# Reordering the RWKV-7 scan pipeline: group norm and gate behind the inverse's first levels, low-rank products ahead of them, fp32 head sums

## The chip, the cores and the metric

The kernel runs on one core of one Trainium2 chip. The metric is device time in microseconds, from the launch's start on the device to its end; lower is better. One execution was also recorded by the hardware profiler.

## What is computed

A two-layer decoder trunk on 16 meta tokens and 256 tokens (272 columns), width 2048, everything in fp32. Layer 0 is RWKV-7 time mixing and a SwiGLU block; layer 1 is stick-breaking attention with a shared K/V and another SwiGLU block. The change lies inside the time mixing:

```python
w = -softplus(-(dec_w0 + tanh(xw @ dec_w1) @ dec_w2)) - 0.5
decay = exp(-exp(w))
a = sigmoid(a_w0 + (xa @ a_w1) @ a_w2)
g = sigmoid(xg @ g_w1) @ g_w2
kk = normalised per head (k * k_k);  k = k * (1 + (a - 1) * k_a)
# per token and head, state 64 x 64
sa    = state @ (-kk)
state = state * decay + sa (kk * a)^T + v k^T
y     = state @ r
# group norm per head, bonus, gate, output projection
y = (y - mean) * rsqrt(var + GN_EPS) * gn_w + gn_b
bonus = sum_head(r * k * r_k) * v
out = ((y + bonus) * g) @ w_o
```

## The kernel before

**Layout.** Activations stand transposed: channels on the 128 partitions, the 272 tokens along the free axis. 2048 channels are 16 slabs, and a slab holds two heads of 64, a "pair". Matrix products against large weights split each fp32 operand into a high and a low part in the reduced format fp32r and add three products (`mm3k`, lines 186 to 188); the weight slabs are split on the chip by a cast on ACT (`whi`, L703) and a subtraction on DVE (`wlo`, L704).

**The scan.** The recurrence is done in chunks: 16 meta tokens, then four chunks of 64. `scan` runs a software pipeline over the 16 pairs, `n` from -3 to 15. In one iteration four pairs are in four different stages:

- C = pair n+3: `lora` (decay and learning rate from the low-rank products, the running decay `L` by a scan on DVE, its exponentials `P`, `Q` and `pe`, then the products `AR0`, `ARV`, `B0`, `BK`).
- B = pair n+2: `chunk0`, `scores`, `neg`, `bonus`, `tokens`, `values`, and `solve`, which inverts the 16 x 16 diagonal blocks on POOL.
- M = pair n+1: `inverse` (two DMA hops through DRAM that bring the solved blocks back as `Tt`), then the two doubling levels `left(16)`, `right(16)`, `left(32)`, `right(32)`, then `apply` and `trans`. `left` transposes `Tt` into `Tn` on DVE and multiplies `yb`; DVE masks it into `Ys`; `right` multiplies `zb` from `Tn` and `Ys`, and DVE adds it to `Tt`.
- A = pair n: `states`, `step(1..4)` (the state passes from chunk to chunk), `norm` (group norm), `gate` (the product `gp` and the output slab `o`).

Between these stages `f(k)` lets PE do k steps of a background stream of large products, one step being the three matmuls of one 128 x 128 weight block (the `w_v` and `w_r` projections of pair n+3, and at the end the first part of `w_o`): 32 steps in a full iteration. While three pairs are left there is no C, and `f` does half as many. The last step of the v projection calls `after_v`, that of the r projection `after_r`.

**What sets the order.** PE and the SP DMA queue run in program order (`manual_schedule`). DVE, ACT and POOL are ordered at compile time by a planner that takes the program's order as priority; each engine then runs its list in that order. One order is written by hand: in `left`

```python
with b.tc.issue_after(b.last.ins):
    V.transpose(self.Tn.rearrange(flat), Tt[:, :4].rearrange(flat))
```

puts the transposition behind the DVE instruction that `b.last` names. `bonus` sets it to its product `bv`, and `gate` sets it again, to the instruction that writes `o`. The order of the calls is `bonus`, `f(2)`, `tokens`, `lora`, `f(3)`, `norm`, `f(1)`, `gate`, `f(3)`, `left(16)`, `values`, `solve`, `f(4)`, `right(16)` and so on.

**Small products.** The per-head sums (`head_sums`: `bonus` and the variance `vb`) multiply a 0/1 block matrix by an operand that ACT and DVE split into high and low first (`high_low`, L996 and L998): two fp32r matmuls each. The low-rank weights of a pair come in two loads (`load_lora`, `load_gate`) and are split where they are used (`split_w`, L989 and L990). PSUM tiles of the scan come from three tags of two banks in rotation (`rbank`). Several SBUF tiles share a buffer through `ALIAS`.

Of the kernel before, what the change touches and what calls it, by code (L numbers as in the profile page):

```python
# [18 lines left out]
NK = D // 128  # L19
# [17 lines left out]
CONST = {}  # L37
ALIAS = {"kk": "ld", "v": "L", "sq": "Mp", "rs2": "Rh", "y": "Ah"}
NRAW = 3
# [79 lines left out]
class Builder:  # L119
# [195 lines left out]
    def vectors(self):  # L315
        nc = self.nc
        self.dvec = {"hdw0": 0, "ha0": NK, "oka": 2 * NK, "mg0": 9 * NK}
        self.dvec.update({f"om{i}": (3 + i) * NK for i in range(6)})
        self.dvec.update(hka=10 * NK, mgn=11 * NK)
# [3 lines left out]
        nc.vector.memset(self.dv[:, b + 2:b + 3], 1.0)  # L323
        self.eps = self.dv[:, b:b + 1]
# [10 lines left out]
        nc.vector.tensor_scalar(self.dv[:, 2 * NK:3 * NK], v16("k_a"), -1.0, 1.0,  # L335
                                ALU.mult, ALU.add)
        o = self.dvec["mgn"]
        nc.vector.tensor_scalar(self.dv[:, o:o + NK], v16("gn_w"), -0.5, None, ALU.mult)
        nc.vector.tensor_scalar(self.dv[:, 3 * NK:9 * NK], self.vecs[:, 0:6 * NK], -1.0, 1.0,
# [8 lines left out]
    def time_mix(self):  # L348
# [13 lines left out]
        with ExitStack() as ctx:  # L362
# [18 lines left out]
            o, n = CONST["blk"]  # L381
            raw = sp.tile([128, 5, 64], F32, name="blk", tag="Tt", bufs=BUFS["Tt"])
            raw = raw.rearrange("p c t -> p (c t)")[:, :n]
            self.dq.dma_start(raw, a["consts"][:, o:o + n])
            self.blk = []
            for i, x in enumerate((1.0, 1.0 / HD)):
                t = sp.tile([128, n], F32R, name="blk", tag=f"blk{i}")
                nc.scalar.activation(t, raw, AF.Copy, scale=x)
                self.blk.append(t)
            with tc.manual_schedule(engines={mybir.EngineType.PE, mybir.EngineType.SP}):  # L390
# [213 lines left out]
    def scan(self, sp):  # L604
# [17 lines left out]

        pairs[0].load_lora()
        for n in range(-3, NK):
            get = lambda i: pairs.get(n + i)
            A, M, B, C = get(0), get(1), get(2), get(3)
            f = fill if C else lambda k: fill(k / 2)
            if M:
                M.inverse()
            if A:  # L630
                A.states()
                A.step(1)
            if B:
                B.chunk0()
            if A:
# [12 lines left out]
            f(2)  # L648
            if B:
                B.tokens()  # L650
            if C:
                C.lora()
            f(3 + (LEAD if n == -3 else 0))
            if A:
                A.norm()
                f(1)
                A.gate()
                f(3)
            else:
                f(4)  # L660
            if M:
                M.left(16)
            if B:
                B.values()
                B.solve()
                if n + 2 == NK - 1:
                    self.rot = self.rot[1:]
            f(4)
            for g in ("right", 16), ("left", 32), ("right", 32), ("apply", None), ("trans", None):
                if M:  # L670
                    getattr(M, g[0])(*g[1:] if g[1] else ())
                f(3 if g[0] == "trans" else 4)
                if g == ("left", 32):
                    if M:
                        M.load_gate()
                    if get(4):
                        get(4).load_lora()

# [267 lines left out]
class Pair:  # L946
# [20 lines left out]

    def load_w(self, lo, hi):

        raw = self.b.l2.tile([128, hi - lo], F32, name="w2", tag="w2", bufs=2)  # L970
        self.nc.sync.dma_start(raw, self.b.a["lora2"][self.p][:, lo:hi])
        return raw

    def load_lora(self):
        p = self.p
        self.da = self.load_w(0, 256)
        self.rn = self.t272("rn")
        self.nc.sync.dma_start(
            self.rn, self.b.rkd[2 * p:2 * p + 2].unsqueeze(1).to_broadcast([2, 64, T]))

    def load_gate(self):
        self.g = self.load_w(256, 512)

    def split_w(self, raw, name):
        b = self.b
        n = raw.shape[1]
        h = b.l2.tile([128, n], F32R, name=name + "h", tag=name + "h", bufs=1)
        l = b.l2.tile([128, n], F32R, name=name + "l", tag=name + "l", bufs=1)
        self.A.copy(h, raw)  # L989
        self.V.tensor_tensor(l, raw, h.bitcast(F32), ALU.subtract)  # L990
        return (h[:, :128], l[:, :128]), (h[:, 128:], l[:, 128:])

    def high_low(self, x):
        b = self.b
        hi = b.rstd_p.tile([128, T], F32R, name="hi", tag="rstd")
        self.A.copy(hi, x)  # L996
        lo = b.rstd_p.tile([128, T], F32R, name="lo", tag="rstdt")
        self.V.tensor_tensor(lo, x, hi.bitcast(F32), ALU.subtract)  # L998
        return hi, lo

    def head_sums(self, name, block, x):

        out = self.b.rbank(name)[:, :T]
        self.PE.matmul(out, block, x[0], start=True, stop=False)
        self.PE.matmul(out, block, x[1], start=False, stop=True)
        return out

    def lora(self):

        b, p, V, A, nc = self.b, self.p, self.V, self.A, self.nc  # L1010
        kt = b.k[p]
        wd, wa = [tuple(x[:96] for x in w) for w in self.split_w(self.da, "da")]
        rn = self.rn
# [10 lines left out]
        A.activation(ta, za[:, :T], AF.Tanh, bias=self.vec("ha0"), scale=0.5)  # L1024

        self.P = P = self.t272("P", 17 + 65 * NCH)
        self.Pc = Pc = P[:, 17:].rearrange("p (c t) -> p c t", t=65)
        nc.gpsimd.memset(P[:, 0:1], 1.0)
        nc.gpsimd.memset(Pc[:, :, 0:1], 1.0)
# [7 lines left out]
        V.tensor_scalar(ta, ta, 0.5, 0.5, ALU.mult, ALU.add)  # L1037
        self.k2 = k2 = self.t272("k2")
# [19 lines left out]
        def par(tile, first, second):  # L1058
# [6 lines left out]
                               Pc[:, :, :C], ALU.mult, ALU.mult)  # L1065
        V.tensor_tensor(kk, ta, kk, ALU.mult)
        V.tensor_tensor(self.B0[:, 0:META], kk[:, :META], Q[:, :META], ALU.mult)
# [4 lines left out]
    def after_v(self, vp):  # L1072
        A = self.A
        self.v = v = self.t272("v")
        A.copy(v, vp)
        self.b.dump("v", self.p, v)
        A.copy(self.V0[:, 32:32 + META], vp[:, :META])
        A.copy(self.ARV[:, :, 2], vp[:, META:].rearrange("p (c t) -> p c t", t=C))

    def after_r(self, rp):  # L1080
        V = self.V
        rs = self.t272("rs")
        self.A.copy(rs, rp)
        V.tensor_tensor(self.AR0[:, 1], rs[:, :META], self.P[:, 1:17], ALU.mult)
        V.tensor_tensor(self.ARV[:, :, 0], rs[:, META:].rearrange("p (c t) -> p c t", t=C),
                        self.Pc[:, :, 1:], ALU.mult)
        V.scalar_tensor_tensor(rs, rs, self.vec("r_k"), self.k2, ALU.mult, ALU.mult)
        self.rk = self.high_low(rs)

# [61 lines left out]
    def bonus(self):  # L1151
        bp = self.head_sums("bonus", self.b.blk[0], self.rk)
        self.bv = self.t272("bv")
        self.b.last = self.V.tensor_tensor(self.bv, self.v, bp, ALU.mult)

# [98 lines left out]
    def apply(self):  # L1254
# [12 lines left out]
        for r in range(2):  # L1267
            self.A.copy(X[HS[r], r * 2:r * 2 + 2, 0], wa4[HS[r], :, :, 1])

# [66 lines left out]
    def gate(self):  # L1336
        b = self.b
        w = self.split_w(self.g, "g")
        gp = b.rbank("gp")
        b.mm3k(gp[:, :T], w[0], b.hg[0], True, False)  # L1340
        b.mm3k(gp[:, :T], w[1], b.hg[1], False, True)
        o = b.kp.tile([128, T], F32, name="o", tag="kp")
        b.last = self.V.scalar_tensor_tensor(o, self.y, self.vec("gn_b"), gp[:, :T], ALU.add, ALU.mult)
        b.dump("o", self.p, o)
# [55 lines left out]
```

## Time and profile before

| | us |
|---|---|
| median of 3 runs (2813.58 to 2815.2) | 2813.61 |
| profiled execution, its own time | 2815.13 |
| span, first to last instruction of it | 2813.3 |
| scan stage, from the first pair's `lora` to the last pair's `o` | about 190 to 748 |

| engine | busy us | share of the span |
|---|---|---|
| PE (matmul) | 2688.5 | 96% |
| DVE | 1798.6 | 64% |
| ACT | 1492.6 | 53% |
| POOL | 178.8 | 6% |

PE is busy nearly all of the time, so a stage can only become shorter where PE waits, where its clock is held down, or where it is given less to do. POOL works in the scan alone, so its row in the table of slices marks that stage. The page's matmul durations overlap, since matmuls are pipelined; the distance of the starts is what one costs.

### The profile page before, as it was taken

The page shows a single profiled execution, that of the slowest core. Times are in us where ns is not written, and L with a number is a line of the kernel's source. Part 1 is how long each engine was busy: PE and PEld are TensorE (multiplying, and loading weights), DVE is VectorE, ACT ScalarE, POOL GpSimd, SP SyncE. Part 2 cuts the span into 40 slices and gives each one's busy share as a digit, 9 for nine tenths or more (in the row PEclk, how much of TensorE's full clock was granted, in tenths as well). Part 3 has the DMA queues.
Part 4 walks back from the last instruction along what each step waited for, and adds up shares of the span by engine and source line. Part 5 has one row for each costly group of instructions (what it writes and reads, how often), then busy time and mean ns, then how long its engine had stood idle before and what let it go on. Part 6 is the DMA issues. An engine that isn't in the chain of part 4 may idle for free.

```text
span 2813.3 us, 54147 instructions
## 1 busy us (share of the span) xinstructions
PE 2688.5 (96%) x20942; PEld 2487.2 (88%) x20942; DVE 1798.6 (64%) x3586; ACT 1492.6 (53%) x3005; POOL 178.8 (6%) x539
## 2 busy tenths in 40 slices
PE   7988888888899999999999999999999999999999
PEld 5777777777799999999999999988888888888888
DVE  6656565566465555555555776577776666666666
ACT  6665555555454444444444665467655455455554
POOL 0005333333100000000000000000000000000000
PEclk9999999999899999999999999999999999999999
DMA  5434333332456555555565555533456565665665
GB/s 177 128 104 122 87 84 84 87 91 78 139 165 186 167 184 176 166 184 177 165 184 177 166 173 165 176 131 116 155 187 187 184 193 180 199 189 179 196 185 175
DMA packets 185330, 439.50 MB, mean 156 GB/s; under 512 B 58448, under 2 KB 88688, under 8 KB 185072
## 3 DMA queue, kind: packets, MB, share of 16 engines
q1 hardware_dynamic: 183488, 433.63, 50.0%
q8 instruction: 164, 2.69, 0.4%
q10 hardware_dynamic: 1584, 2.42, 0.3%
q14 instruction: 94, 0.77, 0.1%
HBM read 430.24 MB, written 5.74 MB: 155 GB/s over the span
## 4 chain that ended last, share of the span: by engine, by line
PE 88%; DVE 4%; ACT 3%; DMA 3%; issue 2%; POOL 0%; SPq 0%; ACTq 0%; DVEq 0%
PE mm L192 22%; PE mm L186 16%; PE mm L188 15%; PE mm L187 15%; PE mm L191 11%; PE lr L540 1%; PE zb L1250 1%; DMA raw<-w_k 1%; DMA raw<-w_r 1%; PE cb L1312 1%; PE hms L831 1%; ACT L1030 1%; PE wa L1261 1%; PE yb L1231 1%; PE cb L1304 1%
## 5 line engine op out<-in xcount | busy, mean ns | idle before, releaser
L168 DVE TENSOR_TENSOR wlo<-raw,whi 128x512 fp32r<-128x512 f32 (+1 forms) x1448 | 979.0, 679 | 621.1 <-ACT whi L167 601.4
L167 ACT CAST whi<-raw 128x512 fp32r<-128x512 f32 (+1 forms) x1448 | 879.3, 610 | 877.0 <-PE mm L187 542.2
L186 PE MATMUL mm<-hl,whi 128*128 128x272 f32 x3344 | 976.1, 292 | 13.4 <-ACT whi L703 9.5
L188 PE MATMUL mm<-hl,wlo 128*128 128x272 f32 x3344 | 968.8, 290 | 4.4 <-DVE wlo L168 4.4
L187 PE MATMUL mm<-hl,whi 128*128 128x272 f32 x3344 | 965.5, 289 | 0.0
L192 PE MATMUL mm<-hl,whi 128*128 128x512 f32 x2624 | 919.8, 395 | 0.0
L191 PE MATMUL mm<-hl,wlo 128*128 128x256 f32 x2624 | 740.8, 282 | 0.0
L186 PEld LDWEIGHTS mm<-hl,whi 128*128 128x128 f32 x3344 | 631.5, 189 | 23.9 <-ACT whi L703 10.0
L187 PEld LDWEIGHTS mm<-hl,whi 128*128 128x128 f32 x3344 | 637.7, 191 | 0.6
L188 PEld LDWEIGHTS mm<-hl,wlo 128*128 128x128 f32 x3344 | 631.8, 189 | 7.1 <-DVE wlo L168 4.8
L192 PEld LDWEIGHTS mm<-hl,whi 128*128 128x128 f32 x2624 | 492.5, 188 | 112.9
L191 PEld LDWEIGHTS mm<-hl,wlo 128*128 128x128 f32 x2624 | 494.2, 188 | 0.6
L704 DVE TENSOR_TENSOR wlo<-raw,whi 128x512 fp32r<-128x512 f32 x140 | 99.1, 715 | 80.6 <-ACT whi L703 79.7
L703 ACT CAST whi<-raw 128x512 fp32r<-128x512 f32 x140 | 86.0, 620 | 62.7 <-PE mm L187 40.1
L208 DVE TENSOR_TENSOR h<-h,mm 128x256 f32<-128x256 f32 (+1 forms) x224 | 93.9, 420 | 6.6 <-PE mm L192 6.0
L1250 PE MATMUL zb<-Ys,Tn 64*64 64x64 f32 x512 | 27.8, 263 | 65.2 <-DVE Tn L1227 60.7
L186 PE MATMUL mm<-hi,whi 128*128 128x272 f32 x256 | 88.9, 347 | 0.0
L1250 PEld LDWEIGHTS zb<-Ys,Tn 64*64 64x64 f32 x512 | 23.1, 170 | 70.8 <-issue 64.0
L187 PE MATMUL mm<-lo,whi 128*128 128x272 f32 x256 | 81.7, 319 | 0.0
L188 PE MATMUL mm<-hi,wlo 128*128 128x272 f32 x256 | 80.9, 316 | 0.0
L201 ACT COPY c<-mm 128x256 f32<-128x256 f32 x104 | 38.7, 373 | 78.8 <-PE mm L192 78.7
L1166 POOL TENSOR_TENSOR Tm<-Ts,As 40x14 f32<-40x14 f32 (+6 forms) x224 | 77.2, 345 | 16.6
(290 smaller groups left out, 2452.4 us busy)
## 6 DMA issues: line engine op xcount, KB each, us to landing
raw<-w_gate SPq DMA_DIRECT2D x176, 512.0 KB
raw<-w_up SPq DMA_DIRECT2D x176, 512.0 KB
raw<-w_down SPq DMA_DIRECT2D x128, 512.0 KB
raw<-w_down SPq DMA_DIRECT2D x128, 192.0 KB
raw<-w_v SPq DMA_DIRECT2D x32, 512.0 KB
raw<-w_r SPq DMA_DIRECT2D x32, 512.0 KB
raw<-sb_w_k SPq DMA_DIRECT2D x32, 512.0 KB
raw<-sb_w_v SPq DMA_DIRECT2D x32, 512.0 KB
```

The source lines that it names most:

```text
L167: nc.scalar.copy(hi, part)
L168: nc.vector.tensor_tensor(lo, part, hi.bitcast(F32), ALU.subtract)
L186: mm(out, w[0], x[0], start=first, stop=False)
L187: mm(out, w[0], x[1], start=False, stop=False)
L188: mm(out, w[1], x[0], start=False, stop=last)
L191: mm(out[:, :n], w[1], x[0], start=first, stop=False, skip_group_check=True)
L192: mm(out, w[0], x[2], start=False, stop=last, skip_group_check=True)
L208: self.nc.vector.tensor_tensor(h, h, out[:, c:c + n], ALU.add)
L703: nc.scalar.copy(hi, part)
L704: nc.vector.tensor_tensor(lo, part, hi.bitcast(F32), ALU.subtract)
L1166: V.tensor_tensor(t, Ts[:, 0:i, i:i + 1].to_broadcast([40, i, n]), As[:, i:i + 1, i + 1:].to_broadcast([40, i, n]), ALU.mult)
L1250: self.PE.matmul(zb[r, i * 64:i * 64 + 64], self.Tn[r, i], self.Ys[r, i], start=True, stop=True)
```

## The change

- The calls are reordered. `solve` follows `scores(1)`; `lora` stands ahead of `bonus`; after `tokens` come six steps of the stream, then `left(16)`, then `norm`, four steps, `right(16)`, `gate`, four steps, `left(32)`, `values`, four steps, `right(32)`, and `apply` and `trans` with four steps behind each. The sum of the steps is 32 as before.
- `gate` no longer sets `b.last`, so the transpositions of `left` are only held behind `bv`.
- `head_sums` is one fp32 matmul; `high_low` is gone, and the block matrices are fp32.
- The low-rank weights of an iteration (gate weights of the next A, decay and rate weights of the next C) go into one 512-wide tile, loaded after `right(32)` of the iteration before and split by one cast and one subtraction at the start of the iteration, the cast behind the last copy of `apply` on ACT.
- `after_v` keeps no copy `v` (`bonus` reads the two other copies, in two products), `after_r` reads PSUM without a copy. The four aliases other than `kk` are gone.
- `P` is one persistent tile whose ones are written once; `pe` is an ACT exponential of four columns of `L` instead of two POOL copies; a factor 1/2 goes into `Q` (a bias of -ln 2), `oka` and `hrk`, so `ta` needs no scaling.

The core of the diff:

```diff
-ALIAS = {"kk": "ld", "v": "L", "sq": "Mp", "rs2": "Rh", "y": "Ah"}
+ALIAS = {"kk": "ld"}
...
+            if A or C:
+                self.split_low(A, C)
...
                 B.scores(1)
+                B.solve()
             if A:
                 A.step(4)
             if B:
                 B.neg()
+            if C:
+                C.lora()
+            if B:
                 B.bonus()
             f(2)
             if B:
                 B.tokens()
-            if C:
-                C.lora()
-            f(3 + (LEAD if n == -3 else 0))
+            f(6 + (LEAD if n == -3 else 0))
+            if M:
+                M.left(16)
             if A:
                 A.norm()
-                f(1)
+            f(4)
+            if M:
+                M.right(16)
+            if A:
                 A.gate()
-                f(3)
+            f(4)
             if M:
-                M.left(16)
+                M.left(32)
             if B:
                 B.values()
-                B.solve()
             f(4)
...
+            if M:
+                M.right(32)
+            self.load_low(M, get(4))
+            f(4)
+            if M:
+                M.apply()
+            f(4)
+            if M:
+                M.trans()
+            f(4)
...
+        hi = self.nc.scalar.copy(h[:, c], self.low[:, c])
...
+            self.tc.add_manual_dep(hi.ins, self.latest.ins.name, nosync,
+                                   reason="weights that land late")
+        self.nc.vector.tensor_tensor(l[:, c], self.low[:, c], h[:, c].bitcast(F32), ALU.subtract)
...
-        self.PE.matmul(out, block, x[0], start=True, stop=False)
-        self.PE.matmul(out, block, x[1], start=False, stop=True)
+        self.PE.matmul(out, block, x, start=True, stop=True)
...
-        nc.gpsimd.tensor_copy(pe[:, 0:1], P[:, 16:17])
-        nc.gpsimd.tensor_copy(pe[:, 1:4], Pc[:, 0:3, 64])
+        A.activation(pe, L[:, META - 1:META + 3 * C:C], AF.Exp)
...
-        A.activation(Q, L, AF.Exp, scale=-1.0)
-        V.tensor_scalar(ta, ta, 0.5, 0.5, ALU.mult, ALU.add)
+        A.activation(Q, L, AF.Exp, scale=-1.0, bias=b.lhalf)
...
-        V.tensor_tensor(kk, ta, kk, ALU.mult)
+        V.scalar_tensor_tensor(kk, ta, 1.0, kk, ALU.add, ALU.mult)
...
-        self.v = v = self.t272("v")
-        A.copy(v, vp)
...
-        rs = self.t272("rs")
-        self.A.copy(rs, rp)
...
-        vb = self.head_sums("vb", self.b.blk[1], self.high_low(sq))
+        vb = self.head_sums("vb", self.b.blk[1], sq)
...
-        w = self.split_w(self.g, "g")
+        w = self.w2
...
-        b.last = self.V.scalar_tensor_tensor(o, self.y, self.vec("gn_b"), gp[:, :T], ALU.add, ALU.mult)
+        self.V.scalar_tensor_tensor(o, self.y, self.vec("gn_b"), gp[:, :T], ALU.add, ALU.mult)
```

More of the change, by code (lines that the diff above doesn't have):

```diff
@@ L334, in vectors @@
             nc.vector.tensor_scalar(self.dv[:, o:o + NK], v16(src), 0.5, None, ALU.mult)
-        nc.vector.tensor_scalar(self.dv[:, 2 * NK:3 * NK], v16("k_a"), -1.0, 1.0,
+        nc.vector.tensor_scalar(self.dv[:, 2 * NK:3 * NK], v16("k_a"), -1.0, 2.0,
                                 ALU.mult, ALU.add)
-        o = self.dvec["mgn"]
-        nc.vector.tensor_scalar(self.dv[:, o:o + NK], v16("gn_w"), -0.5, None, ALU.mult)
+        for dst, src, c in (("hrk", "r_k", 0.5), ("mgn", "gn_w", -0.5)):
+            o = self.dvec[dst]
+            nc.vector.tensor_scalar(self.dv[:, o:o + NK], v16(src), c, None, ALU.mult)
         nc.vector.tensor_scalar(self.dv[:, 3 * NK:9 * NK], self.vecs[:, 0:6 * NK], -1.0, 1.0,
@@ L381, in time_mix @@
             o, n = CONST["blk"]
[L382 to L389, printed above, removed]
+            self.blk = [sp.tile([128, n], F32, name="blk", tag=f"blk{i}") for i in range(2)]
+            self.dq.dma_start(self.blk[0], a["consts"][:, o:o + n])
+            nc.scalar.activation(self.blk[1], self.blk[0], AF.Copy, scale=1.0 / HD)
+            self.P = sp.tile([128, 17 + 65 * NCH], F32, name="P", tag="P")
+            nc.gpsimd.memset(self.P[:, 0:1], 1.0)
+            nc.gpsimd.memset(self.P[:, 17:].rearrange("p (c t) -> p c t", t=65)[:, :, 0:1], 1.0)
             with tc.manual_schedule(engines={mybir.EngineType.PE, mybir.EngineType.SP}):
@@ L621, in fill @@
                 next(stream, 0)
-        pairs[0].load_lora()
+        self.latest = None
+        self.load_low(None, pairs[0])
         for n in range(-3, NK):
@@ L650, in scan @@
                 B.tokens()
-            if C:
-                C.lora()
-            f(3 + (LEAD if n == -3 else 0))
+            f(6 + (LEAD if n == -3 else 0))
+            if B and n + 2 == NK - 1:
+                self.rot = self.rot[1:]
+            if M:
+                M.left(16)
             if A:
                 A.norm()
-                f(1)
+            f(4)
+            if M:
+                M.right(16)
+            if A:
                 A.gate()
-                f(3)
-            else:
-                f(4)
+            f(4)
@@ L661, in scan @@
             if M:
-                M.left(16)
+                M.left(32)
             if B:
                 B.values()
-                B.solve()
-                if n + 2 == NK - 1:
-                    self.rot = self.rot[1:]
-            f(4)
[L669 to L677, printed above, removed]
+            f(4)
@@ new lines, in scan, with load_low @@
+            if M:
[8 more added lines that the diff above has]
+            f(4)
+    def load_low(self, A, C):
+        if not (A or C):
+            return
+        nc, a = self.nc, self.a
+        self.low = self.l2.tile([128, 512], F32, name="w2", tag="w2", bufs=2)
+        if C:
+            p = C.p
+            nc.sync.dma_start(self.low[:, :256], a["lora2"][p][:, :256])
+            C.rn = C.t272("rn")
+            nc.sync.dma_start(C.rn, self.rkd[2 * p:2 * p + 2].unsqueeze(1).to_broadcast([2, 64, T]))
+        if A:
+            nc.sync.dma_start(self.low[:, 256:], a["lora2"][A.p][:, 256:512])
@@ new lines, in split_low @@
+    def split_low(self, A, C):
+        c = slice(0 if C else 256, 512 if A else 256)
+        h = self.l2.tile([128, 512], F32R, name="w2h", tag="w2h", bufs=1)
+        l = self.l2.tile([128, 512], F32R, name="w2l", tag="w2l", bufs=1)
+        hi = self.nc.scalar.copy(h[:, c], self.low[:, c])
+        if self.latest:
+            nosync = mybir.DependencyInfo(mybir.DependencyClass.NoSync, mybir.DependencyReason.DATA)
+            self.tc.add_manual_dep(hi.ins, self.latest.ins.name, nosync,
+                                   reason="weights that land late")
+        self.nc.vector.tensor_tensor(l[:, c], self.low[:, c], h[:, c].bitcast(F32), ALU.subtract)
+        for x, o, r in (C, 0, 96), (A, 256, 128):
+            if x:
+                x.w2 = [(h[:r, i:i + 128], l[:r, i:i + 128]) for i in (o, o + 128)]
@@ L1011, in lora @@
         kt = b.k[p]
-        wd, wa = [tuple(x[:96] for x in w) for w in self.split_w(self.da, "da")]
+        wd, wa = self.w2
         rn = self.rn
@@ L1081, in after_r @@
         V = self.V
[L1082 to L1085 removed]
+        V.tensor_tensor(self.AR0[:, 1], rp[:, :META], self.P[:, 1:17], ALU.mult)
+        V.tensor_tensor(self.ARV[:, :, 0], rp[:, META:].rearrange("p (c t) -> p c t", t=C),
                         self.Pc[:, :, 1:], ALU.mult)
[L1087 to L1088 removed]
+        self.rk = self.t272("rs")
+        V.scalar_tensor_tensor(self.rk, rp, self.vec("hrk"), self.k2, ALU.mult, ALU.mult)
     def chunk0(self):
@@ L1153, in bonus @@
         self.bv = self.t272("bv")
-        self.b.last = self.V.tensor_tensor(self.bv, self.v, bp, ALU.mult)
+        self.V.tensor_tensor(self.bv[:, :META], self.V0[:, 32:32 + META], bp[:, :META], ALU.mult)
+        c4 = lambda x: x[:, META:].rearrange("p (c t) -> p c t", t=C)
+        self.b.last = self.V.tensor_tensor(c4(self.bv), self.ARV[:, :, 2], c4(bp), ALU.mult)
     def solve(self):
```

38 lines of the change are left out of this document (5 added, 33 removed).

## Prediction

> **What bounds the kernel now.** I read the page first (busy shares, slices), then busy time and clock by stage, then the waits inside the scan, then the order of time on PE and DVE around the largest wait.
>
> ```profile
> span 2813.3 us, 54147 instructions
> PE 2688.5 (96%) x20942; PEld 2487.2 (88%) x20942; DVE 1798.6 (64%) x3586; ACT 1492.6 (53%) x3005; POOL 178.8 (6%) x539
> ```
>
> PE is the bound. What can be won by new order lies where PE stands still or runs slowly. By stretches (length, then busy us of PE, PEld, DVE, ACT and POOL, granted clock, DMA share, GB/s):
>
> ```profile
> 405.06:438.28 33.22, 28.39 (x360) 25.44 (x360) 20.39 (x52) 17.45 (x42) 10.93 (x34) 0.91 0.35 89
> 205.60:272.30 66.70, 57.50 (x715) 51.73 (x715) 44.44 (x111) 36.94 (x96) 30.71 (x85) 0.98 0.43 121
> 272.30:706.00 433.70, 371.77 (x4681) 332.85 (x4679) 263.48 (x648) 228.17 (x548) 139.76 (x422) 0.91 0.33 86
> 706.00:748.00 42.00, 34.84 (x412) 29.78 (x408) 17.12 (x42) 16.35 (x34) 6.38 (x19) 0.90 0.15 39
> 434.30:437.55 3.25, 0.01 (x1) 0.00 (x0) 3.25 (x9) 1.51 (x5) 2.66 (x8) 1.00 0.06 23
> 437.55:444.37 6.82, 5.51 (x49) 5.06 (x50) 4.35 (x10) 1.33 (x3) 5.57 (x17) 0.50 0.73 207
> ```
>
> The first row is one iteration of the scan: 33.22 us, PE idle for 4.83 of them. The last two show where: PE does nothing from 434.3 while DVE is busy throughout, and behind that the clock is at 0.50 for 6.82 us. The first 66.7 us of the scan, which hardly have a pair in `norm`, keep 0.98. The waits of the scan (us in total, times, longest) and the order of time around one of them:
>
> ```profile
> ACT gh L989 <- DMA w<-lora: 61.2, 13, 5.5
> PE zb L1250 <- DVE Tn L1227: 60.7, 14, 4.6
> PE zb L1250 <- ACT hl L249: 4.5, 1, 4.5
> PE bonus L1004 <- DVE G L1123: 3.1, 14, 0.2
> ```
>
> ```profile
> 433.37 0.44 DVE L1066 TENSOR_TENSOR kk<-ta,kk 128x272 f32<-128x272 f32 x1
> ...
> 434.91 0.41 DVE L1236 TENSOR_TENSOR Ys<-yb,consts 128x256 f32<-128x256 f32 x1
> ...
> 436.75 0.51 DVE L1334 SCALAR_TENSOR_TENSOR y<-y,dv,bv 128x272 f32<-128x272 f32 x1
> 437.18 0.76 DVE L704 TENSOR_TENSOR wlo<-raw,whi 128x512 fp32r<-128x512 f32 x1
> 437.87 0.48 DVE L1343 SCALAR_TENSOR_TENSOR o<-y,vecs,gp 128x272 f32<-128x272 f32 x1
> 438.28 0.43 DVE L1227 STREAM_TRANSPOSE Tn<-Tt 128x256 f32<-128x256 f32 x1
> 438.86 1.12 PE L1250 MATMUL zb<-Ys,Tn 64*64 64x64 f32 x16 [4.54 <-DVE Tn L1227]
> ```
>
> PE's product `zb` of `right(16)` waits for `Tn`, whose other input `Ys` was there at 435.3. `Tn` is held behind `o`, the end of the whole norm and gate of another pair, and DVE comes to that late since `lora` of a third pair stands ahead. So 15 times 4.3 us: 60.7 + 4.5 = 65.2 us.
>
> **The change part by part.**
>
> *The wait at `zb`.* `b.last` is now `bv`, which is ahead of the fills, and norm and gate come later. Between `yb` and `zb` PE now has `vb` and four steps, 2 us, in which DVE only needs `Ys` (0.41). Gain 65.2.
>
> *The clock.* With no standstill of 4.5 us I expect no fall to 0.50. At a clock of 0.91 over 433.7 us the loss is 0.09 x 433.7 = 39 us; I take all of it. The 0.98 of the early stretch, where PE also idles for 9.2 us in all but in small pieces, is the evidence. [...]
>
> *Head sums as fp32.* Costs of matmuls by the distance of starts:
>
> ```profile
> 433.52 0.29 PE L187 MATMUL mm<-hl,whi 128*128 128x272 f32 x1
> ...
> 433.77 0.29 PE L186 MATMUL mm<-hi,whi 128*128 128x272 f32 x1
> ...
> 119.64 4.59 PE L540 MATMUL lr<-xi,raw 128*96 128x272 f32 x19
> ...
> L540 PE MATMUL lr<-xi,raw 128*96 128x272 f32 (+1 forms) x128 | 30.3, 395 | 0.0
> ```
>
> The first two rows are two fp32r matmuls apart: one of 272 columns costs 0.125 us, so one step of the stream 0.375. At L540 fp32 matmuls run: 64 in the code, 128 records, so two records each, of 4.59/19 = 0.24 us: 0.48 for one. A head sum goes from 0.25 to 0.48; 2 x 16 of them cost 7.4 us, all on PE.
>
> *What leaves ACT, DVE and POOL.* Per iteration:
>
> ```profile
> L996 ACT CAST hi<-sq 128x272 fp32r<-128x272 f32 x16 | 6.8, 422 | 0.0
> L998 DVE TENSOR_TENSOR lo<-sq,hi 128x272 fp32r<-128x272 f32 x16 | 7.1, 443 | 9.0 <-ACT hi L996 9.0
> L1083 ACT COPY rs<-mm 128x272 f32<-128x272 f32 x16 | 6.2, 384 | 0.3
> L1075 ACT COPY v<-mm 128x272 f32<-128x272 f32 x15 | 5.8, 385 | 0.8 <-PE mm L188 0.8
> L1037 DVE TENSOR_SCALAR ta<-ta 128x272 f32<-128x272 f32 x15 | 4.1, 276 | 0.0
> ```
>
> ACT: two casts (0.84) and two copies (0.77) go, the four-column `pe` comes (I take 0.2, under the 0.43 of the 272-column Exp below): -1.4, from 17.45 to 16.0. DVE: two subtractions (0.88) and `ta` (0.28) go, a second, short product of `bv` comes and one 512-wide split takes the place of two of 256 (I let these two cancel; each is under the 0.44 of a 272-column operation): -1.2, from 20.39 to 19.2. In an iteration of 26.7 us (below) that is 60% and 72%, so neither becomes the bound, and nothing of it is counted; the cover is PE's own work. Reading `mm` in PSUM on DVE costs me nothing: at 512 columns `G<-ba` reads PSUM in 0.68 us (below), `wlo<-raw,whi` SBUF in 0.76 (above). POOL's two memsets and two copies were covered and stay worth nothing; the solve is bound by its own chain.
>
> *Queues that the moved steps pass.* The loads of the low-rank weights go four steps later on SP, 128 KB each as before, and their cast on ACT moves from the middle of one iteration to the start of the next. That takes away ACT's standstill of 61.2 us. The new cover is worked out at the fourth rival. `solve` and the inverse's DMAs:
>
> ```profile
> 424.13 0.68 DVE L1123 TENSOR_TENSOR G<-ba,consts 128x512 f32<-128x512 f32 x1
> ...
> 444.88 0.30 SPq L1174 DMA_DIRECT2D s<-Ts  x1
> 446.96 1.27 SPq L1177 DMA_DIRECT2D Tt<-s  x2
> ...
> 234.72 2.52 DMA Tt<-s
> ```
>
> From `G` to `Tt` in SBUF it takes 448.2 + 2.5 (the first pair's landing) - 424.8 = 25.9 us. In iterations of 26.7 us `Tt` lands 0.8 us ahead of the end of the next `G`. `Tn` may start once `bv` is done: `neg` ends 0.8 us before `G` (rows below), then come `lora` (six matmuls, 0.75), `bonus` (0.48) and `bv` (0.4), so 0.8 to 1.2 us after `G`. `yb` follows eight steps (3.0) and `tokens` later still. Cover is left, but 2 us for `Tn` where an iteration of 33.2 gave 6.5 more. SP stands at `inverse` until POOL is done and issues weight loads late; six buffers of four blocks each are split ahead, 24 steps or 9 us, so I put nothing.
>
> *What is late next.* (a) `lora` now follows `neg` at once, and its first bank comes free only after ACT's `y` or DVE's `G`:
>
> ```profile
> 423.58 0.46 PE L1145 MATMUL b<-BK,ARV 64*64 64x64 f32 x16
> ...
> 424.09 0.38 ACT L1320 COPY y<-cb 128x272 f32<-128x272 f32 x1
> ```
>
> `neg` ends at 424.04, `y` at 424.47: at most 0.43 us, and 0.2 by the old wait at `bonus`. I take 0.3 x 16 = 5 us; the old wait (3.1) goes.
>
> (b) `left(32)` needs `Tt<-Tt,zb` on DVE, and norm's five products (five times 0.43) may stand ahead of it. Norm now has its Ln and Exp in a row, as only the last pairs had:
>
> ```profile
> 695.97 1.28 ACT L1328 ACT_TABLE_LOAD   x1
> 697.27 0.49 ACT L1328 ACTIVATE rs<-vb,dv 128x272 f32<-128x272 f32 x1
> 697.77 1.28 ACT L1329 ACT_TABLE_LOAD   x1
> 699.06 0.43 ACT L1329 ACTIVATE rs<-rs 128x272 f32<-128x272 f32 x1
> ```
>
> Counting from the end of `vb`: 0.49 + 1.28 + 0.43 = 2.2 us if the first load runs ahead, then 2.2 us of DVE: the sum for `Tt` would be done at 4.8. PE reaches `left(32)` after four steps, `zb`, `gp` (six matmuls) and four steps, 1.5 + 0.56 (half of `zb`'s 1.12 at half clock) + 0.75 + 1.5 = 4.3. A wait of 0.5, or of 0 if the planner puts the sum first, or of 1.9 if two weight splits (0.7 each) stand there too. I take 0.5 x 15 = 7.5 us, the case nearest to norm's own rows; the ends are 0 and 28.
>
> [...]
>
> *Sum.* -65.2 - 39 + 7.4 - 3.1 + 5 + 7.5 = -87. The profiled execution's own time is 2815.1 (span 2813.3), 1.5 above the median 2813.6. 2815.1 - 87 = **2728 us**. An iteration would be 33.2 - 4.54 - 3.0 + 0.46 + 0.6 = 26.7 us. Runs of this kernel differ by up to 0.06%, so about 0.2% (5.6 us) can be told from no change.
>
> **The rivals.**
>
> 1. *The wait moves.* DVE reaches the sum for `left(32)`, or `Tn` waits in DVE's list for a `Tt` that lands late, 2.5 us in each of 15 iterations. For: in the quoted stretch DVE is full, and norm's ACT chain is in its way. Against: DVE has 28% to spare. With the clock free: 2728 - 7.5 + 37.5 = 2758. If such waits still pull the clock down, 39 more: 2797; the only length that the rows show at a fall is 4.54, so this half gets less. [...]
> 2. *All of it is hidden.* No new waits at all and the clock free to the end of the scan (42 us at 0.90 from 706): 2815.1 - 65.2 - 39 - 3.1 - 4 + 7.4 = 2711.
> 3. *Nothing changes.* The planner leaves `Tn` behind norm on DVE though nothing forces it: 2815 + 7 = 2822 with the head sums, 2815 where the lighter ACT pays for them. Against: norm's input `vb` is now only produced after `yb`.
> 4. *Slower.* The cast of the low-rank weights stands on ACT ahead of the state copies `S` of `step`, and PE's steps wait for these in order. If the load lands late, PE stands. This decides from (65.2 + 39 + 3.1 - 7.4)/16 = 6.2 us of wait per iteration. For: ACT waited up to 5.5 us for these loads. Against: the load was issued at 404.0 and used at 407.9,
>
> ```profile
> 404.01 0.90 SPq L971 DMA_DIRECT2D w<-lora  x2
> ...
> 407.85 0.41 ACT L989 CAST gh<-w 128x256 fp32r<-128x256 f32 x1 [5.26 <-DMA w<-lora]
> ```
>
>    3.9 us later, and now has at least twelve steps (4.5 us), `apply` and `trans` to land. At 8 us of wait per iteration: 2815 + 16 x 1.8 = 2844.
>
> **How the numbers follow.** Chances: the forecast 0.60 (2718 to 2748), everything hidden 0.10, the wait moves with a free clock 0.14, with a held clock 0.06, nothing changes 0.04, slower 0.06. The forecast is the likeliest. The range from 2705 (rival 2 and a little) to 2768 leaves out the last three and the far end of the third. Faster: 0.60 + 0.10 + 0.14 + 0.06 = 0.90; same 0.04; slower 0.06.
>
> **What would show it.** Right: no wait of `zb` for `Tn`, iterations of 26 to 27.5 us by the distance of the `Tn`, a clock of 0.98 or more from 272 to the scan's end, `bonus` and `vb` with two records each, no wait of ACT on `w<-lora`. The next waits should be `yb` on `Tt` L1251 and `zw` on its bank. Wrong: a clock still at 0.9, waits of PE over 2 us at `yb`, `zb` or `cb`, or a DVE near 90% in the scan.

## The result and the profile after

| | us | ratio to before |
|---|---|---|
| before, median of 4 runs beside it | 2814.34 (2813.58 to 2815.2) | |
| after, median of 4 runs | 2738.03 (2735.73 to 2740.69) | 0.9729, interval 0.9712 to 0.9746 |
| forecast | 2728 (2705 to 2768) | |

The change saves 76 us where the forecast had 87. The profiled execution of after took 2735.7 us, 79 less than that of before. The page of the changed kernel begins:

```profile
span 2733.9 us, 53852 instructions
PE 2666.4 (98%) x20942; PEld 2464.4 (90%) x20942; DVE 1771.0 (65%) x3543; ACT 1470.0 (54%) x2943; POOL 167.0 (6%) x477
PEclk9999999998999999999999999999999999999999
```

PE has the same number of matmul records, since a fp32 head sum takes two of them, as the two fp32r products did (32 records of `bonus` for 16 pairs, in both). PE is busy 22 us less in all and idle 57 us less. The stretch of full iterations of after, and one iteration from `Tn` to `Tn` (same columns as in the prediction: length, busy us of PE, PEld, DVE, ACT, POOL, clock, DMA share, GB/s):

```profile
272.30:640.00 367.70, 355.30 (x4780) 313.88 (x4776) 244.68 (x623) 213.37 (x509) 137.84 (x388) 1.00 0.35 102
423.98:451.50 27.52, 26.84 (x362) 23.79 (x361) 18.40 (x49) 16.02 (x38) 10.33 (x29) 1.00 0.36 108
```

The same stretch of before:

```profile
272.30:640.00 367.70, 314.47 (x3962) 281.87 (x3959) 223.63 (x550) 191.88 (x461) 120.61 (x364) 0.91 0.33 87
```

In equal time PE gets through 4780 matmul records instead of 3962. An iteration, the mean distance of the first `Tn` from one to the next between 271 and 639 us, went from 33.44 to 27.52 us. The surroundings of `zb` of `right(16)` in that iteration of after, in the order of time:

```profile
424.25 0.44 DVE L1224 STREAM_TRANSPOSE Tn<-Tt 128x256 f32<-128x256 f32 x1
...
429.23 0.42 DVE L1233 TENSOR_TENSOR Ys<-yb,consts 128x256 f32<-128x256 f32 x1 [0.31 <-PE yb L1231]
...
431.27 0.68 PE L1247 MATMUL zb<-Ys,Tn 64*64 64x64 f32 x16
432.00 0.42 DVE L1248 TENSOR_TENSOR Tt<-Tt,zb 128x256 f32<-128x256 f32 x1 [2.21 <-PE zb L1247]
433.60 0.44 DVE L1327 TENSOR_TENSOR sq<-rs 128x272 f32<-128x272 f32 x1 [1.18 <-ACT rs L1326]
```

`Tn` is done 6.6 us ahead of `zb`, and `zb` has no wait. The norm's products begin only at 433.60, behind the sum for `Tt`. The waits of PE in the scan that are left (us in total, times, longest):

```profile
PE mm L186 <- ACT whi L741: 9.3, 1, 9.3
...
PE zb L1247 <- DVE Ys L1233: 3.0, 13, 0.3
PE zw L186 <- DVE G L1118: 2.9, 13, 0.2
...
PE wa L1258 <- DVE Tt L1248: 1.9, 8, 0.6
...
PE yb L1228 <- DMA Tt<-s: 1.7, 2, 1.4
```

The first is the wait for the scan's first weights, which the kernel before has too.

### The profile page after: what moved, and what is told of

Its sections match the earlier page's. It is cut to its first block, busy times and chain, and to the rows that moved or that the text cites. A ratio compares the mean times of both kernels' runs of the same rounds, so it can differ in the third digit from the quotient of the medians.

```text
span 2733.9 us, 53852 instructions
## 1 busy us (share of the span) xinstructions
PE 2666.4 (98%) x20942; PEld 2464.4 (90%) x20942; DVE 1771.0 (65%) x3543; ACT 1470.0 (54%) x2943; POOL 167.0 (6%) x477
## 4 chain that ended last, share of the span: by engine, by line
PE 75%; DVE 0%; issue 0%
PE mm L192 22%; PE mm L186 13%; PE mm L188 13%; PE mm L187 13%; PE mm L191 11%; PE hms L869 1%; PE z L946 1%; PE lt L959 0%; PE op L970 0%; PE tbv L938 0%; PE op L971 0%; PE lt L960 0%; PE lt L962 0%; PE ms L801 0%; PE op L972 0%; DVE h L208 0%
## 5 line engine op out<-in xcount | busy, mean ns | idle before, releaser
L186 PEld LDWEIGHTS mm<-hl,whi 128*128 128x128 f32 x3344 | 632.0, 189 | 27.5 <-ACT whi L741 9.8
L186 PE MATMUL mm<-hi,whi 128*128 128x272 f32 x256 | 78.3, 306 | 0.0
L1165 POOL TENSOR_TENSOR Ts<-Ts,Tm 40x14 f32<-40x14 f32 (+6 forms) x224 | 74.9, 334 | 17.5
L187 PE MATMUL mm<-lo,whi 128*128 128x272 f32 x256 | 73.8, 288 | 0.0
L188 PE MATMUL mm<-hi,wlo 128*128 128x272 f32 x256 | 73.5, 287 | 0.0
L186 PEld LDWEIGHTS mm<-hi,whi 128*128 128x128 f32 x256 | 48.1, 188 | 4.4 <-issue 2.4
```

Source lines behind the costliest of these rows:

```text
L186: mm(out, w[0], x[0], start=first, stop=False)
L187: mm(out, w[0], x[1], start=False, stop=False)
L188: mm(out, w[1], x[0], start=False, stop=last)
L1165: V.tensor_tensor(Ts[:, 0:i, i + 1:], Ts[:, 0:i, i + 1:], t, ALU.add)
```

## The experiments

All times are medians. The kernel before, run beside them, had 2814.9 us with `b_last`, `b_order`, `a_fp32r` and `a_lora`, 2816.5 with `b_warm`, `b_hold_y`, `b_hold_rs` and `a_copies`, and 2815.3 with `b_warm24`, `a_best` and `a_best_warm`.

### Releasing `Tn` alone, and together with the new order

`b_last` is the kernel before with one line changed:

```diff
-        b.last = self.V.scalar_tensor_tensor(o, self.y, self.vec("gn_b"), gp[:, :T], ALU.add, ALU.mult)
+        self.V.scalar_tensor_tensor(o, self.y, self.vec("gn_b"), gp[:, :T], ALU.add, ALU.mult)
```

> The kernel before with one line changed: the gate no longer sets the instruction behind which the transposition Tn is held. Theory 1 (the hold is the cause): Tn goes right behind bv on DVE, zb then waits for Ys alone, about 1.0 us instead of 4.5, and the clock comes back: 2815 - 15 x 3.5 - 39 = 2724, 2715 to 2745. Theory 2 (the fewer copies and splits and the later loads carry the gain): at most a third of it, 2790 or more. Theory 3 (DVE is too full at that place, Ys takes over): zb waits 2.5 us or more, 2750 to 2785.

Measured: 2741.73 us, ratio 0.974 (0.9727 to 0.9753). PE's largest wait and the stretch:

```profile
PE zb L1250 <- DVE Ys L1236: 15.7, 13, 1.7
```

```profile
272.30:640.00 367.70, 344.89 (x4727) 306.99 (x4725) 262.68 (x653) 226.84 (x553) 157.11 (x434) 1.00 0.36 100
```

This line alone brings 73 of the 76 us. DVE still works through the whole norm in that place, but `Tn` no longer stands behind it; 1.15 us of wait for `Ys` stay in each iteration, and the clock is free.

`b_order` is the kernel before with that line and the new place of norm, gate, `left`, `right` and `values`. `lora` stays behind `tokens`, `solve` behind `values`, and the fp32r head sums and the copies are as before; the low-rank weights still come in two loads, but these are issued behind `right(32)`:

```diff
+            f(3)
...
+            if M:
+                M.left(16)
             if A:
                 A.norm()
-                f(1)
+            f(4)
+            if M:
+                M.right(16)
+            if A:
                 A.gate()
-                f(3)
...
+            f(4)
             if M:
-                M.left(16)
+                M.left(32)
```

> The kernel before with the new order of norm, gate, left and right alone: lora stays behind tokens, the low-rank weights come in two loads with two splits (loaded after right(32)), head sums stay two fp32r products with their splits, all copies and aliases stay. Theory 1 (order carries the gain): no fp32 cost, so 2738 - 7 = 2731 or somewhat less, 2715 to 2745. Theory 2 (copies, splits, aliases matter): 2770 or more, with PE waiting in trans or apply where the aliased tiles hold norm's values.

Measured: 2738.89 us, ratio 0.9727 (0.9714 to 0.9741). Against `b_last` 2.8 us less, with intervals that overlap: the move of norm and gate itself, beside the released `Tn`, is worth 3 us or nothing. The wait for `Ys` is smaller in sum and at most 0.9 us long:

```profile
PE zb L1257 <- DVE Ys L1243: 10.7, 23, 0.9
```

The new order with the hold left in was not run. In it `left(16)` comes ahead of `gate`, so only the transposition of `left(32)` would still stand behind `o`; whether the order without the released line would have brought the same gain is not shown.

### Undoing other parts of the change

`a_fp32r`: after, with the head sums as two fp32r products of a high and a low part again.

```diff
-        self.PE.matmul(out, block, x, start=True, stop=True)
+        self.PE.matmul(out, block, x[0], start=True, stop=False)
+        self.PE.matmul(out, block, x[1], start=False, stop=True)
...
-        vb = self.head_sums("vb", self.b.blk[1], sq)
+        vb = self.head_sums("vb", self.b.blk[1], self.high_low(sq))
```

> The changed kernel with the head sums as two fp32r products with high and low parts again. Theory 1 (the fp32 product costs PE 0.23 us each and nothing hides it): 2738 - 7.4 = 2731, 2727 to 2734. Theory 2 (the casts on ACT and the subtractions on DVE come back into norm's chain and cost as much): 2736 to 2746, with longer waits of PE at zb, wa or zw.

Measured: 2731.23 us, ratio 0.9699 (0.9686 to 0.9712), 6.8 below after, with an iteration of 27.2 instead of 27.5 us. The fp32 head sums are a loss of the size forecast.

`a_lora`: after, with `lora` behind `tokens` again.

```diff
-            if C:
-                C.lora()
...
                 B.tokens()
+            if C:
+                C.lora()
```

> The changed kernel with lora back behind tokens, everything else as changed. Theory 1 (its place is not what matters; PE has the same work): 2734 to 2743. Theory 2 (ahead of bonus it gives DVE time; behind tokens DVE is full when yb is done and zb waits for Ys 1 to 2 us in 15 iterations): 2753 to 2768.

Measured: 2742.89 us, ratio 0.9744 (0.9731 to 0.9758), 4.9 above after. The two intervals overlap, but in the traces the full iterations of `a_lora` take 27.88 to 28.02 us and those of after 27.22 to 27.69. The early `lora` is worth some 5 us, where the forecast had only a cost for it (5 us at its bank, 3.1 of them back at `bonus`). What PE waited for is not what I expected (`zb` on `Ys`), but the next product, `wa`, on the last sum for `Tt`:

```profile
PE wa L1258 <- DVE Tt L1248: 6.9, 12, 0.7
```

`a_copies`: after, with the copies through ACT and POOL and the single product `bv` put back.

```diff
+        self.v = v = self.t272("v")
+        A.copy(v, vp)
...
+        rs = self.t272("rsc")
+        self.A.copy(rs, rp)
```

> The kernel after, with the copies put back: v and the removal's product through ACT into SBUF, bv as one product over that copy, the four columns pe as two copies on POOL. ACT gets 0.8 us more in an iteration of 27.5 us in which it is busy 58%. Theory (PE is the bound and ACT and POOL have slack): 0 to +3 us, 2738 to 2741. Rival (ACT's place in line sets the bank's release and b's wait): 0.4 us in each of 16 iterations, about 2744.

Measured: 2738.35 us, ratio 0.9725 (0.9711 to 0.974): the same as after. Fewer copies bring nothing; ACT and POOL had room for them.

### What the slow clock costs, and at what wait it sets in

In the kernel before, clock and wait came together. `b_warm` keeps the wait and takes away the standstill: PE multiplies data that nobody uses while it waits.

```diff
 def right(self, s):
+        b = self.b
+        if s == 16 and self.p >= 1:
+            dm = b.rbank("dm")[:, :T]
+            w = b.hg[0][0]
+            for i in range(32):
+                self.PE.matmul(dm, w[:, :128], w, start=True, stop=True)
```

> The kernel before, with 32 matmuls of 272 columns (fp32r, of data that is there) put into a bank that nobody reads, just ahead of zb in right(16) of all pairs but the first, where PE stands still for 4.55 us. Tn still waits behind o. The 32 take about 32 x 0.125 = 4.0 us, all of it inside the standstill. Theory (the slow clock of 0.50 behind each wait comes from PE standing still, and is worth 2.36 us of an iteration by the distance from b_last to before): the granted clock goes from 0.91 to 0.99 or more in the scan, and the time falls by 13 x 2.36 = 31 us, to about 2784. Rival (the clock term as I forecast it, 3.0 us in each of 13 iterations): 2775. Rival (the clock has nothing to do with standing still): no change, 2814, or more by what the 32 stick out.

Measured: 2789.17 us, ratio 0.9903 (0.9889 to 0.9918).

```profile
455.27 4.17 PE L1252 MATMUL dm<-hg0h 128*128 128x272 f32 x32
460.00 0.68 PE L1256 MATMUL zb<-Ys,Tn 64*64 64x64 f32 x16 [0.55 <-DVE Tn L1227]
```

```profile
272.30:640.00 367.70, 357.90 (x4619) 324.86 (x4620) 238.69 (x588) 205.62 (x495) 131.12 (x382) 1.00 0.34 92
```

`zb` comes as late behind its inputs as before (0.55 us of wait behind 4 us of idle products), the clock is 1.00, and 27 us are gone. The iteration is 31.27 instead of 33.44 us. So the slow clock was worth 2.2 us of an iteration, and it came from the standstill.

`b_hold_y` and `b_hold_rs` hold `Tn` behind an earlier product of the norm, for a shorter wait; the first is

```diff
-        V.scalar_tensor_tensor(y, y, self.vec("mgn"), self.bv, ALU.mult, ALU.add)
+        self.b.last = V.scalar_tensor_tensor(y, y, self.vec("mgn"), self.bv, ALU.mult, ALU.add)
```

and the second does the same with `rs2` two products earlier. In both, `gate` no longer sets the hold.

> The kernel before, with Tn held behind the norm's last product y instead of behind the gate's o: DVE gets to Tn one product and one split of weights earlier, so PE's wait at zb should be 3.2 to 3.6 us instead of 4.55. If such a wait still pulls the clock down: clock 0.91 to 0.93, the time 2814 - 13 x 1.1 = 2800. If it leaves the clock free: clock 0.99 or more and 2814 - 13 x (1.1 + 2.36) = 2769. In between if only some of the 13 are long enough.

> The kernel before, with Tn held behind the norm's second product rs2: two further products earlier, a wait at zb of 2.0 to 2.6 us. If the clock falls only at waits of three or more: clock 0.99 or more and 2814 - 13 x (2.2 + 2.36) = 2755. If it falls at any wait of this kind: clock 0.91 to 0.93 and 2814 - 13 x 2.2 = 2785.

Measured: `b_hold_y` 2796.47 us, ratio 0.9931 (0.9916 to 0.9946), waits of 3.45 us, clock 0.93 from 272.3 to 640. `b_hold_rs` 2761.0 us, ratio 0.9808 (0.9792 to 0.9824), waits of 1.87 us, clock 0.96. The first is the case "still pulls the clock down"; the second lies between its two, because only some of the waits do: its iterations are either 28.55 or 30.0 us long. The stretch from 272.3 to 640, of `b_hold_y` and then of `b_hold_rs`:

```profile
272.30:640.00 367.70, 325.54 (x4139) 291.67 (x4141) 231.85 (x575) 198.28 (x478) 132.10 (x386) 0.93 0.35 92
272.30:640.00 367.70, 341.70 (x4517) 305.31 (x4515) 252.19 (x631) 217.76 (x529) 145.25 (x410) 0.96 0.37 97
```

Where they differ shows in stretches of 3.41 us of `b_hold_rs`, two waits of the same length:

```profile
411.84:415.25 3.41, 1.54 (x24) 1.32 (x22) 3.41 (x12) 2.44 (x8) 2.70 (x10) 1.00 0.31 125
415.25:418.66 3.41, 3.41 (x23) 3.11 (x20) 2.73 (x6) 0.62 (x1) 2.86 (x8) 0.50 0.15 20
418.66:422.07 3.41, 3.41 (x52) 3.12 (x49) 2.62 (x5) 0.93 (x2) 2.94 (x7) 1.00 0.92 236
473.28:476.69 3.41, 1.83 (x25) 1.79 (x26) 3.41 (x12) 1.77 (x5) 2.70 (x10) 1.00 0.39 160
476.69:480.10 3.41, 3.41 (x53) 3.04 (x51) 3.34 (x7) 1.55 (x3) 2.94 (x7) 1.00 0.43 121
```

The slow stretch begins at 415.3 and is 3.41 us long, and the seven other slow ones between 272 and 640 begin whole multiples of 3.413 us from it (the first at 326.5, 26 of them before, the last at 623.5, 61 behind). The rows are cut on these multiples. In the kernel before, too, the slow times between 270 and 646 us are 3.41 or 6.83 us long, and each begins 9 or 10 times 3.413 us behind the last. In the rows a stretch with PE busy for 1.54 us was followed by one at 0.50, a stretch with 1.83 was not: the wait of 1.87 us lay whole in the first, and a boundary cut it in the second case. One slow stretch cost 1.47 us of an iteration (30.02 - 28.55).

Busy time alone does not tell which stretches were followed by a slow one, though. Two stretches of after, cut in the same way from the start of its slow time at 636.75, then two of `a_best_warm`, cut from that of its slow time at 665.81:

```profile
633.33:636.75 3.42, 2.18 (x34) 1.70 (x33) 0.00 (x0) 1.57 (x5) 1.19 (x6) 1.00 0.13 14
636.75:640.16 3.41, 2.05 (x11) 1.70 (x9) 0.00 (x0) 0.04 (x1) 0.00 (x0) 0.50 0.27 62
...
679.46:682.87 3.41, 1.58 (x13) 1.36 (x11) 3.41 (x10) 3.41 (x10) 0.00 (x0) 1.00 0.81 288
682.87:686.29 3.42, 3.40 (x25) 3.25 (x26) 3.42 (x7) 1.64 (x3) 0.00 (x0) 1.00 0.50 158
```

In after 2.18 us of work, mostly small products of 64 x 64 (`cb`), were followed by a slow stretch; in `a_best_warm` 1.58 us of the stream's 128 x 128 products were not. What made the difference is not shown.

In the kernel before, a wait of 4.55 us left PE busy for 0.00 to 1.09 us of one such stretch, and the slow stretch behind it was often followed by a second: the slow time in the prediction, 6.82 us from 437.55, is two of them. Between 270 and 646 us a second one followed in the ten cases in which PE was busy for 1.19 to 2.88 us of the first, and none in the two with 3.04 and 3.06.

`b_warm24` tests whether a shorter wait leaves the clock free: the same as `b_warm` with 24 idle products, so a wait of 1.55 us. The windows of the theory below are the stretches of 3.41 us above, and its 1.8 us is my estimate from the rows of `b_hold_rs` (1.87 us without work ahead of a slow stretch, 1.58 ahead of a free one). No run shows that the clock is judged so, and the stretch of after above, with 1.24 us without work and a slow one behind it, does not fit.

```diff
-            for i in range(32):
+            for i in range(24):
```

> b_warm with 24 idle products instead of 32: PE's wait at zb for Tn should be 4.55 - 24 x 0.125 = 1.55 us. Theory (the clock is judged in fixed windows of 3.41 us, and falls for the next window when PE stood still for more than about 1.8 us, half of one): no window behind these waits is slow, clock 0.99 or more, the time as b_warm's, 2789. Rival (any wait above some 1.5 us pulls the clock down): 13 x 1.71 = 22 us more, about 2811. Between the two if only some of the waits do.

Measured: 2784.61 us, ratio 0.9893 (0.9879 to 0.9906), waits of 1.55 us, the same iteration of 31.27 us as `b_warm`, clock 1.00 in

```profile
272.30:640.00 367.70, 347.08 (x4542) 314.11 (x4541) 240.02 (x594) 209.09 (x507) 131.21 (x382) 1.00 0.35 92
```

No stretch between 272 and 640 was slow. So these waits of 1.55 us left the clock free; where a limit lies is not shown. The rival (a fall at any wait above 1.5 us, 2811 us) is out.

### Two attempts at more

`a_best` is `a_fp32r` with the products put in the order `neg`, `tokens`, `lora`, `bonus` and all eight steps behind:

```diff
+            if B:
+                B.tokens()
...
-            f(2)
-            if B:
-                B.tokens()
-            f(6 + (LEAD if n == -3 else 0))
+            f(8 + (LEAD if n == -3 else 0))
```

The expectation puts 0.2 us on a change of format. In after the fp32r product behind the fp32 `bonus` starts 0.32 us ahead of the next one (423.43 to 423.75), where the ones behind it start 0.125 apart; no run shows that as a cost of the format by itself.

> a_fp32r (head sums as two fp32r products) with the order neg, tokens, lora, bonus, f(8), so that lora's products and the bonus stand together and no fp32 product is between fp32r ones there, and lora comes when its bank has long been free. Theory (PE is the bound; zw's wait of 0.2 us and one change of format fall away): 0.4 us in each of 16 iterations, 2731 - 6 = 2725. Rival (lora later makes Tn or Ys late, as in a_lora): 2731 or up to 2736.

Measured: 2731.51 us, ratio 0.9706 (0.9693 to 0.9719): nothing gained on `a_fp32r`. From the first to the last `Tn` it takes 409.0 us, `a_fp32r` 408.7. The 0.2 us at `zw` are paid again by `tb`, whose bank now waits for the same `G`:

```profile
PE tb L1197 <- DVE G L1132: 3.1, 14, 0.2
```

`a_best_warm` adds idle products where PE stands still at the scan's ends:

```diff
+                if p == 0 and acts is self.xv:
+                    self.keep_busy(out, acts[0][0], 66)
...
+        self.keep_busy(self.rbank("dm")[:, :T], self.hg[0][0], 24)
...
+        if s == 16 and self.p == NK - 1:
+            b.keep_busy(yb[:, :T], b.hg[0][0], 12)
```

> a_best with idle products (fp32r, into banks whose content is overwritten after) where PE stands still at the ends of the scan: 66 (8.25 us) ahead of the scan's first large product, which waits 9.46 us; 12 ahead of yb in left(16) of the last pair (wait 2.46 us), 24 ahead of the output projection's second part (wait 3.48 us). Theory (the slow windows there come from standing still): in a_fp32r they lose 5.07, 1.71, 3.41 and 1.71 us; I expect 8 to 11 us less than a_best, about 2716. Rival (the waits are longer behind them, or these windows are slow for another reason): the same as a_best within 2 us.

Measured: 2735.26 us, ratio 0.9723 (0.971 to 0.9736), not faster. At the scan's start they did free the clock. The stretch in which PE stands and restarts, in `a_best`:

```profile
181.50:191.75 10.25, 3.74 (x15) 3.42 (x16) 7.15 (x18) 5.33 (x13) 0.00 (x0) 0.50 0.51 182
```

The same in `a_best_warm`, where the idle products fill it:

```profile
178.00:186.80 8.80, 8.50 (x66) 8.06 (x64) 5.07 (x14) 6.05 (x14) 0.00 (x0) 1.00 0.74 221
```

But the first `Tn` comes at 231.66 us instead of 231.63: it and PE's `yb` behind it wait for the first pair's `Tt`, which comes by DMA. At the scan's end PE waited up to 8.3 us instead of 3.3 for the output projection's weights:

```profile
PE mm L186 <- ACT whi L167: 10.1, 2, 8.3
```

The traces show what came between. The first loads of these weights are issued at 656.96 in `a_best`, ahead of loads of `h`; in `a_best_warm` at 663.80, behind loads of `h` that had waited on the same queue for `o`:

```profile
656.96 1.85 SPq L156 DMA_DIRECT2D raw<-w_o  x4
660.32 2.65 SPq L819 DMA_DIRECT2D h<-xT  x4
...
660.99 2.70 SPq L826 DMA_DIRECT2D h<-xT  x6
663.80 2.72 SPq L156 DMA_DIRECT2D raw<-w_o  x4
```

So the run changed the order on the SP queue as well, and the clock fell there all the same, for 10.24 us from 665.81. What idle products alone would bring at the scan's end is not shown, and why the order on SP changed stays open.

The best version measured is `a_fp32r` (2731.2 us, 6.8 below after), with `a_best` equal to it.

## Why the prediction was right, and where its size was off

*The wait at `zb`* went as forecast: 65.2 us of waits for `Tn` and `hl` are gone, 3.0 for `Ys` came. That is -62 of the -65. That the hand-written hold makes this wait, and not the load on DVE, is shown by `b_last`.

*The clock* is the term that was mis-sized: 39 us forecast, 27 measured (`b_warm`), 2.2 instead of 3.0 in each iteration. The working took the lost clock share times the whole time, which counts too much twice. First, a slow stretch can begin while PE still stands: of the 6.82 us at 0.50 from 437.55, PE was busy for 5.51, and the other 1.31 were counted in the wait already. Second, at 0.50 the stream's products do not take twice as long. In that stretch ten products take 2.26 us from start to start, 0.226 for one against 0.125 at 1.00, so a busy microsecond loses 0.45 and not 0.5:

```profile
440.30 0.43 PE L187 MATMUL mm<-lo,whi 128*128 128x272 f32 x1
...
442.56 0.43 PE L188 MATMUL mm<-hi,wlo 128*128 128x272 f32 x1
```

In the eleven falls from 270 to 612 us PE was busy for 56.3 us of the slow time, 5.1 in each, and 5.1 x 0.45 = 2.3, close to the 2.2 measured. That the clock would come back to 1.00 was right for the full iterations; from 636.75 on after still has 20.5 us at 0.50, as the kernel before has slow stretches at its scan's end.

*The head sums*: 7.4 us forecast, 6.8 measured. The distance of starts in after, 0.58 us from `bonus` to the second product behind it, 0.125 of which is the first one's, gives 0.455 for one sum, where 0.48 was forecast:

```profile
423.17 0.62 PE L1009 MATMUL bonus<-rs,blk 128*128 128x272 f32 x2
423.43 0.49 PE L186 MATMUL mm<-hl,whi 128*128 128x272 f32 x1
423.75 0.29 PE L187 MATMUL mm<-hl,whi 128*128 128x272 f32 x1
```

*What is late next.* (a) `zw` waits 2.9 us in all where 5 was forecast, and takes the place of the 3.1 at `bonus`. (b) The 7.5 us for `left(32)` did not come: the planner put the sum for `Tt` first, one of the three cases named; 1.9 us at `wa`, which the sum did not have, came in its place. The norm's chain on ACT has its first table load run ahead and a second one between Ln and Exp, as forecast; but two copies stand between them, and from the end of `vb` (429.84) to the end of the Exp it takes 3.7 us instead of 2.2:

```profile
427.70 1.28 ACT L1325 ACT_TABLE_LOAD   x1
429.87 0.49 ACT L1325 ACTIVATE rs<-vb,dv 128x272 f32<-128x272 f32 x1 [0.89 <-PE vb L1009]
431.84 1.28 ACT L1326 ACT_TABLE_LOAD   x1
433.13 0.43 ACT L1326 ACTIVATE rs<-rs 128x272 f32<-128x272 f32 x1
```

With the sum put ahead of the chain, none of the waits of PE that are left is for a product of the norm.

*The copies* at nothing were right (`a_copies`). *The place of `lora`* was only half seen: the sum gives it a cost at its bank and nothing for what it saves, and undone alone it costs 5 us (`a_lora`). It is no term that is missing in the sum, since the sum counts the waits that after has.

*The sum with measured terms*: -62 (wait) - 27 (clock) + 6.8 (head sums) - 3.1 + 2.9 (`bonus` and `zw`) + 1.9 (`wa`) = -80.5, so 2815.1 - 80.5 = 2734.6 against 2735.7 of the profiled execution. Against the forecast, the clock adds 12 us and the wait for `Ys` 3; the wait at `left(32)` gives back 5.6, the smaller one at `zw` 2.1 and the head sums 0.6; 1 us stays open. That the forecast came so close is in part luck, since terms that were put too high on both sides cancel.

*The signs.* Iterations of 27.5 us lie at the upper edge of the 26 to 27.5 named. `zw` waits for its bank, as named; the named wait of `yb` on the sum for `Tt` does not appear, and `zb` on `Ys` and `wa` on `Tt` stand there instead. DVE is busy for 67% of the stretch.

*The rivals.* "The wait moves" was forecast at 2.5 us in each iteration; what is left in after is 0.3 at most for `Ys` and once 0.7 for `o` at `zb`, 0.6 at `wa`, and two waits of `yb` for `Tt` by DMA, the longer 1.4. "All of it is hidden" would have been 2711 and was too low mostly by the clock: 12 us as above and 4 for a scan end that it let run at the full clock. "Nothing changes" is out: `Tn` no longer stands behind norm. "Slower" is out: ACT's 61 us of standstill on the load of `w` are gone, and PE waits for no copy `S` longer than 0.4 us.

## What to carry to other kernels

Look first for an ordering that is written by hand and what it holds up: of a change of many parts, one line alone gave 73 of 76 us, and one part (fp32 head sums) took 7 away. When a wait and a slow clock come together, the cost of the clock is what PE loses while it is working; count slow time by PE's busy time in it (here 5.51 of 6.82 us), and not by the whole stretch. In `b_hold_rs` a wait of 1.87 us cost nothing or 1.47 us more than its length, in `b_hold_y` one of 3.45 us up to some 2.6 (32.75 us for the longer iterations against 28.55 - 1.87 + 3.45 = 30.1 with a free clock). In the full iterations of `b_warm24`, waits of 1.55 us cost only their length: the clock stayed at 1.00.

## What the runs showed of the hardware

- In the full iterations of `b_hold_rs` the clock fell to 0.50 for stretches of 3.41 us that began whole multiples of 3.413 us apart. It fell behind a stretch in which PE was busy for 1.54 us, and stayed at 1.00 behind one with 1.83. I had thought of the length of the wait; equal waits of 1.87 us in one execution had different prices. Busy time alone does not settle it: 2.18 us, mostly of small products, were followed by a slow stretch in after, and 1.58 us of full ones were not in `a_best_warm`.
- At a granted clock of 0.50 the starts of the 272-column products were 0.226 us apart, against 0.125 at 1.00.
- With 24 idle products in a wait of 4.55 us the clock stayed at 1.00 in `b_warm24`, and an iteration took 2.2 us less, though 1.55 us of standstill remained.
